# The end of a convolution in a two-layer backbone: its transforms, its adaLN units and its waits put in another order by hand

## The chip, the cores and the metric

The kernel runs on one core of one Trainium2 chip. The metric is device microseconds of one execution; a time shown is the median of the runs that it stands for. A core has a matrix engine (TensorE, PE in the profile, with its weight loads listed as PEld), a vector engine (VectorE, DVE), a scalar engine (ScalarE, ACT), a general engine (GpSimd, POOL) and an engine that here only issues loads (SyncE, SP). Each engine works through its own list of instructions in order. Matrix results land in PSUM, of which this kernel uses eight banks; everything else is in the on-chip memory SBUF, and weights come from device memory by DMA.

## The reference

The reference takes 256 latent tokens and 256 context tokens of width 1024 through two layers. Both layers have the form

```
sh1, sc1, g1, sh2, sc2, g2 = split(silu(c) @ ada_w[i] + ada_b[i], 6)      # adaLN
u = h * (1 + sc1) + sh1
h = LN(ALPHA * h + g1 * mixer(u))
h = LN(ALPHA * h + g2 * (relu(mod(h, sh2, sc2) @ w1) ** 2 @ w2))
```

for the latent stream with c and for the context stream with a learned vector. The mixer of layer 1 is a bidirectional mLSTM. The mixer of layer 0, where the change is, is a Conformer convolution:

```
a = u @ w_pw1 + b_pw1                     # 1024 -> 2048
a = a[:, :1024] * sigmoid(a[:, 1024:])
a = dwconv(a, w_dw)                       # 31 taps along the tokens; the latents in rows of 64
a = silu(LN(a + b_dw))
y = a @ w_pw2 + b_pw2
```

All inputs and outputs are float32.

## The kernel before

The 512 tokens are the columns of most tiles: context first, latents behind. A float32 product is made of three matmuls of shortened operands: each weight tile is split into a high part (a cast on ScalarE, L153) and a low part (a subtraction on VectorE, L154), and `mm3` (L175 to L180) multiplies high by high, high by low and low by high.

A planner lays out the program. It goes through the instructions in the order in which the code states them, which is their priority, gives each to its engine when its own model of the times says that its inputs are there, and adds the waits. So an engine's list can differ from the order of the code. Two means steer it: `tc.issue_after(x)` puts what is stated inside the block behind instruction x on x's engine, and `tc.high_priority(-100)` makes a block less urgent. Tiles of a kind (a tag) share a fixed number of buffers; a tile waits until one is free. PSUM has three banks "mm", two "ln", one "fl" and two "cv". Weights arrive in `raw` (three buffers of 1 MB, L149).

The convolution runs as follows.

- **Start.** The first adaLN quantities and four of pw1's sixteen output blocks are made together, feature block by feature block (`start0` to `start2`). Loads and small results use `F`, five buffers of 128x512.
- **Tables.** A block of low priority builds sine tables (L650 to L690) on VectorE, loads the row `bdw` (L705), and defines `taps`, which loads the 31 taps of one half of the channels into an F buffer (L710) and makes their spectra Hc and Hs with two matmuls of 31 rows (L713).
- **pw1.** `gemm_steps` (L218) makes the other twelve blocks, m = 0 to 11, two to a 1 MB load. After block m it calls `pw1_next(m)`. An even m gives a gate (a sigmoid on ScalarE, L761). An odd m gives a value, which VectorE multiplies by the gate (L765); PE transposes the result (L768) and ScalarE copies it into A (L769). Eight of these blocks, counting the first four, make 1024 channels; channels 0 to 511 are complete after m = 3, the others after m = 11.
- **Spectral filter.** `spectral(h, tt)` takes half h of the channels and one of four tiles tt of 128 tokens: two forward transforms (L788 for the context tiles 0 and 1, L794 for the latent tiles 2 and 3, where each is a 64-row matmul and the two can share the array), four products with Hc and Hs on VectorE (L805, L806), and an inverse transform of four matmuls in two pairs of 64 columns (L826), then the bias on VectorE (L833) and token statistics (L834). In the profile a float32 matmul is two records, so a whole inverse transform is x8.
- **Token norm.** `token_norm(pair)` turns the statistics of two tiles into a scale and a shift with a chain of small operations on VectorE (L839 to L847), and ScalarE applies them to the four half tiles (L851).
- **silu.** `silu(s)` transposes the two tiles of a stream back (L903), applies the activation (L905) and splits the result; pw2 consumes it. The context stream comes first.
- **adaLN units.** The remaining adaLN columns of layer 0 come in units of 512 columns, 2 MB each, as 8 products of 32 columns of the array (`ada_mm`, L334; 16 records), each on one of four column groups that run side by side. `Ada` collects units in the bank "fl": `ada_g1` units 4 and 5, `ada_s2` units 6 to 9, with a copy to SBUF behind the last (L374) and a fold into place (`end`, L342, L379). Before the change unit 4 and 5 come at m = 3 and 5, units 6, 7 and 8 at m = 7, 9 and 11 and unit 9 behind pw1; the first half of unit 8 lies in four small tiles loaded early (L883).

Behind pw1, before the change, `pw1_epi` states the second half's tiles 0 and 1 and the norm of that pair, then come unit 9, the context's silu, tiles 2 and 3 with a part of the products held back behind the norm, and the norm of the second pair.

## Time and profile before

| what | value |
|---|---|
| median of 3 runs | 1713.19 us |
| lowest and highest of them | 1710.81 and 1713.68 us |
| profiled execution | 1711.69 us |
| its span in the profile | 1709.9 us |
| mean granted clock of PE | 0.996 |
| PE busy | 1680.3 us, 98% of the span |
| VectorE busy | 1032.3 us, 60% |
| ScalarE busy | 746.2 us, 44% |
| instructions | 22801 |

The profile is one execution. The span goes from its first to its last instruction; the time of the execution is a little longer. Matmuls are pipelined and their ends are modelled, so two of them may overlap in the list, and a busy PE is not PE at its peak. The chain of work that ended last is followed back from the last instruction, at each step to what released it or to the instruction ahead of it on its engine; in order of time each row gives the start, the length, the engine with the tile and line, and how many instructions were merged. In a timeline, brackets give the engine's idle time before the row and who ended it. The waits list who waited for whom: total, times, longest. SPq rows are DMA issues. In the rows of busy time by stretches, the clock is the share of full speed that was granted to PE. Line numbers are those of the kernel before.

### The profile page before, as it was taken

What the parts mean: (1) busy time and instruction counts of PE and PEld (TensorE: products, weight loads), DVE (VectorE), ACT (ScalarE), POOL (GpSimd) and SP (SyncE); (2) the same over time, 40 slices, a digit from 0 to 9 for tenths busy, and PEclk for the clock granted to TensorE, in tenths of its full rate; (3) what the DMA queues carried; (4) which work ended last, traced back from release to release, by engine and by line L of the source; (5) the groups of instructions that cost most, each with busy time, mean ns of one, the idle gap of its engine ahead of it and who ended that gap; (6) DMA issues with size and microseconds to landing.
All of it is one profiled execution on the core that took longest, in us unless ns stands there. A gap on an engine that the chain in (4) does not pass through costs nothing.

```text
span 1709.9 us, 22801 instructions
## 1 busy us (share of the span) xinstructions
PE 1680.3 (98%) x8886; PEld 1365.5 (80%) x8886; DVE 1032.3 (60%) x1840; ACT 746.2 (44%) x1198; POOL 44.3 (3%) x92
## 2 busy tenths in 40 slices
PE   7999999999999999999999999999999999999997
PEld 5655798887888998876688899888877878878886
DVE  5554785666645675762144554464387776776677
ACT  3312664232324366652232542442467564545453
POOL 0000000000000000000000000000011120000001
PEclk9999999999999999999999999999999999999999
DMA  8436224443423155568675753355454556766552
GB/s 346 169 123 225 77 75 172 147 143 123 148 105 124 50 163 189 182 220 278 231 227 173 248 190 123 130 203 179 138 207 154 197 194 208 257 222 225 193 181 91
DMA packets 70396, 300.53 MB, mean 176 GB/s; under 512 B 7123, under 2 KB 21971, under 8 KB 39825
## 3 DMA queue, kind: packets, MB, share of 16 engines
q1 hardware_dynamic: 52624, 284.39, 47.4%
q10 hardware_dynamic: 17664, 14.69, 2.6%
q8 instruction: 70, 1.15, 0.3%
q14 instruction: 38, 0.30, 0.0%
HBM read 283.32 MB, written 15.73 MB: 175 GB/s over the span
## 4 chain that ended last, share of the span: by engine, by line
PE 92%; DVE 4%; ACT 1%; issue 1%; DMA 1%; POOL 0%; SPq 0%; DVEq 0%; ACTq 0%; POOLq 0%
PE mm L176 17%; PE mm L179 17%; PE mm L180 17%; PE mm L189 7%; PE mm L190 3%; PE mm L205 3%; PE mm L206 3%; PE mm L207 3%; PE cv L207 2%; PE cv L205 2%; PE cv L206 2%; PE fl L334 2%; DVE wl L154 1%; PE cv L826 1%; PE fl L739 1%
## 5 line engine op out<-in xcount | busy, mean ns | idle before, releaser
L154 DVE TENSOR_TENSOR wl<-raw,wh 128x1024 fp32r<-128x1024 f32 x346 | 424.5, 1233 | 273.9 <-ACT wh L153 271.3
L153 ACT CAST wh<-raw 128x1024 fp32r<-128x1024 f32 x346 | 360.3, 1050 | 492.3 <-PE mm L179 256.8
L179 PE MATMUL mm<-u,wh 128*128 128x512 f32 (+1 forms) x824 | 297.1, 361 | 0.0
L176 PE MATMUL mm<-u,wh 128*128 128x512 f32 (+1 forms) x696 | 248.6, 358 | 0.8 <-ACT wh L153 0.5
L180 PE MATMUL mm<-u,wl 128*128 128x512 f32 (+1 forms) x696 | 246.9, 355 | 0.0
L179 PEld LDWEIGHTS mm<-u,wh 128*128 128x128 f32 x824 | 156.0, 189 | 22.9 <-issue 1.3
L176 PEld LDWEIGHTS mm<-u,wh 128*128 128x128 f32 x696 | 131.6, 190 | 30.1 <-issue 5.7
L180 PEld LDWEIGHTS mm<-u,wl 128*128 128x128 f32 x696 | 131.8, 189 | 19.3 <-issue 1.3
L176 PE MATMUL mm<-xm,wh 128*128 128x512 f32 x256 | 102.2, 399 | 0.0
L205 PE MATMUL mm<-wh,xl 128*128 128x512 f32 x256 | 101.4, 397 | 0.5 <-ACT wh L153 0.5
L206 PE MATMUL mm<-wh,xl 128*128 128x512 f32 x256 | 100.9, 394 | 0.0
L180 PE MATMUL mm<-xm,wl 128*128 128x512 f32 x256 | 99.9, 390 | 0.0
L207 PE MATMUL mm<-wl,xl 128*128 128x512 f32 x256 | 99.6, 392 | 0.0
L176 PE MATMUL mm<-hid,wh 128*128 128x512 f32 (+1 forms) x256 | 93.1, 364 | 0.0
L179 PE MATMUL mm<-hid,wh 128*128 128x512 f32 (+1 forms) x256 | 92.8, 363 | 0.0
L180 PE MATMUL mm<-hid,wl 128*128 128x512 f32 (+1 forms) x256 | 92.7, 362 | 0.0
L189 PE MATMUL mm<-x,wh 128*128 128x512 f32 x232 | 81.0, 398 | 0.8 <-DVE x L1649 0.8
L410 DVE SCALAR_TENSOR_TENSOR S<-ar,cs,S 128x512 f32<-128x512 f32 x56 | 40.8, 749 | 64.7 <-DMA ar<-ada_w 64.6
L179 PE MATMUL mm<-qq,wh 128*128 128x272 f32 x256 | 73.9, 289 | 0.0
L176 PE MATMUL mm<-qq,wh 128*128 128x272 f32 x256 | 73.5, 288 | 0.0
L180 PE MATMUL mm<-qq,wl 128*128 128x272 f32 x256 | 73.5, 288 | 0.0
L189 PE MATMUL mm<-u,wh 128*128 128x512 f32 x192 | 68.6, 399 | 0.0
(506 smaller groups left out, 3270.1 us busy)
## 6 DMA issues: line engine op xcount, KB each, us to landing
raw<-w SPq DMA_DIRECT2D x64, 1024.0 KB, 4.8
raw<-wo SPq DMA_DIRECT2D x32, 1024.0 KB, 4.9
raw<-ada_w SPq DMA_DIRECT2D x27, 1024.0 KB, 5.0
ar<-ada_w SPq DMA_DIRECT2D x80, 256.0 KB, 3.8
raw<-wv SPq DMA_DIRECT2D x16, 1024.0 KB, 7.3
raw<-wqT SPq DMA_DIRECT2D x16, 1024.0 KB, 5.2
raw<-wq SPq DMA_DIRECT2D x16, 1024.0 KB, 5.1
raw<-wk SPq DMA_DIRECT2D x16, 1024.0 KB, 4.9
```

The source lines that it names most:

```text
L153: c = nc.scalar.copy(hi, src)
L154: nc.vector.tensor_tensor(lo, src, hi.bitcast(F32), op=ALU.subtract)
L176: a = nc.tensor.matmul(ps, wh, xh, start=start, stop=False)
L179: nc.tensor.matmul(ps, wh, xl, start=False, stop=False)
L180: nc.tensor.matmul(ps, wl, xh, start=False, stop=stop)
L189: todo = [lambda s_, e_: nc.tensor.matmul(ps, wh, r[0], start=s_, stop=e_), lambda s_, e_: nc.tensor.matmul(ps[:, :n], wl, r[0][:, :n], st ...
L190: lambda s_, e_: nc.tensor.matmul(ps[:, :n], wl, r[0][:, :n], start=s_, stop=e_)]
L205: nc.tensor.matmul(ps, xh, wh, start=start, stop=False)
L206: nc.tensor.matmul(ps, xl, wh, start=False, stop=False)
L207: nc.tensor.matmul(ps, xh, wl, start=False, stop=stop)
L334: a = nc.tensor.matmul(ps[32 * j:32 * j + 32], cs[:, kt, 14 - 2 * v:46 - 2 * v], blocks[kt], start=first and kt < 4, stop=last and kt >= 4 ...
L410: nc.vector.scalar_tensor_tensor(a, w, c, a, op0=ALU.mult, op1=ALU.add)
```

## The change

It leaves the arithmetic as it is, but for the engine that does two steps, and orders the work around the end of the convolution.

- The two tap loads move out of `taps` into the low-priority block of tables.
- `spectral` is taken apart into `fwd`, `products` (one half tile's two products a call) and `back`. For the first half of the channels they are called in the old order.
- For the second half the order is written out behind pw1: the first half of unit 9 behind the last transposes, the forward transforms of tiles 0 and 1, the inverse of 0 behind them, the forward of 2, the inverse of 1, the norm of the pair, the second half of unit 9. Within the silu of the context follow the second products of tile 2 behind the norm, its inverse and the forward of 3 behind the fourth transpose, and the inverse of 3 behind the sixth.
- Unit 4 is done in two halves around the transposes of m = 3; units 5, 6 and 7 come at m = 4, 6 and 8, each behind the last matmul of that block.
- The copy of `ada_s2` goes from VectorE to ScalarE. The token norm is applied to the pair's second tile by VectorE, to the first by ScalarE.

```diff
+    wds = [F()[:NTAP, :] for _ in range(2)]
+    for h_ in range(2):
+        nc.sync.dma_start(wds[h_], wdw_d[0:NTAP, h_ * 512:(h_ + 1) * 512])
     def taps(h_):
-        wd = F()[:NTAP, :]
-        nc.sync.dma_start(wd, wdw_d[0:NTAP, h_ * 512:(h_ + 1) * 512])
+        wd = wds[h_]
...
+                if self is ada_s2:
+                    nc.scalar.copy(self.sb, self.ps)
+                else:
+                    nc.vector.tensor_copy(self.sb, self.ps)
...
         if f == 3:
+            with tc.issue_after(mark["tr"]):
+                ada_g1.mm(first, range(4, 8))
             for tt in range(4):
-                spectral(0, tt)
-        if f == 7:
-            for tt in range(2):
-                spectral(1, tt)
-            token_norm(0)
+                fwd(0, tt, [psum() for _ in range(2)])
+                products(0, tt)
+                products(0, tt)
+                back(0, tt, psum("cv"))
...
-            for i in range(2):
-                y = Y[2 * pair + i][h]
-                nc.scalar.activation(y, y, AF.Identity, scale=mv[:, i, 2:3], bias=mv[:, i, 3:4])
+            y, z = [Y[2 * pair + i][h] for i in range(2)]
+            nc.scalar.activation(y, y, AF.Identity, scale=mv[:, 0, 2:3], bias=mv[:, 0, 3:4])
+            mark["norm", h] = nc.vector.tensor_scalar(z, z, mv[:, 1, 2:3], mv[:, 1, 3:4], op0=ALU.mult, op1=ALU.add).ins
...
     def pw1_next(m, ps):
+        if m == 3:
+            first.extend(ada_load(0, 4))
+            ada_g1.mm(first, range(4))
...
-        if m in Z.fd[:2]:
-            ada_g1.mm(ada_load(0, 4 + ada_g1.n))
-        if m == Z.fd[2]:
+        if m in (4, 6, 8):
+            unit = ada_g1 if m == 4 else ada_s2
+            blocks = ada_load(0, unit.u0 + unit.n)
+            with tc.issue_after(lastmm[0]):
+                unit.mm(blocks)
+        if m == 5:
             ada_g1.end()
-        if m in (7, 9):
-            ada_s2.mm()
-        if m == 9:
+        if m == 8:
...
     last = ada_load(0, 6 + ada_s2.n)
-    with tc.issue_after(mark["fwd", 1, 0]):
-        ada_s2.mm(last)
+    with tc.issue_after(mark["tr"]):
+        ada_s2.mm(last, range(4))
+    for tt in range(2):
+        fwd(1, tt, [psum() for _ in range(2)])
+    cv = [psum("cv") for _ in range(2)]
+    products(1, 0)
+    products(1, 0)
+    with tc.issue_after(mark["fwd", 1]):
+        back(1, 0, cv[0])
+    products(1, 1)
+    products(1, 1)
+    xb = [psum() for _ in range(2)]
+    fwd(1, 2, xb)
+    with tc.issue_after(mark["fwd", 2]):
+        back(1, 1, cv[1])
+    products(1, 2)
+    token_norm(0)
+    with tc.issue_after(mark["fwd", 2]):
+        ada_s2.mm(last, range(4, 8))
...
-    lead2 = [psum() for _ in range(2)]
-    banks = [psum(), psum("cv"), psum("cv")]
-    for tt in (2, 3):
-        spectral(1, tt, banks)
+    lead2 = [psum(), psum("cv")]
+    ob = psum("cv")
+    with tc.issue_after(mark["norm", 0]):
+        products(1, 2)
+    with tc.issue_after(mark["turn", 3]):
+        back(1, 2, ob)
+        fwd(1, 3, xb)
+    products(1, 3)
+    products(1, 3)
+    with tc.issue_after(mark["turn", 5]):
+        back(1, 3, ob)
     token_norm(1)
     ada_s2.end()
```

`mark["tr"]` is the last transpose of a value block, `mark["turn", f]` the last transpose of feature block f in the silu, `mark["fwd", tt]` the last forward matmul of a tile, and `lastmm[0]` the matmul that `mm3` stated last.

More of the change, by code (lines that the diff above doesn't have):

```diff
@@ L32 @@
 class Z:
-    fd = [3, 5, 6]
     wq0 = 2
@@ L179, in mm3 @@
         nc.tensor.matmul(ps, wh, xl, start=False, stop=False)
-        nc.tensor.matmul(ps, wl, xh, start=False, stop=stop)
+        lastmm[0] = nc.tensor.matmul(ps, wl, xh, start=False, stop=stop).ins
+    lastmm = [None]
     def mm_any(ps, wh, wl, r, start, stop):
@@ L329, in hybrid_kernel, with ada_mm @@
     ada = [con.tile([P, 48, 2], F32, name=f"ada{l}") for l in range(2)]
-    def ada_mm(ps, blocks, v=0, first=True, last=True):
-        for kt in range(DT):
+    def ada_mm(ps, blocks, v=0, first=True, last=True, kts=range(DT)):
+        for kt in kts:
             j = kt % 4
@@ L364, in __init__, with mm @@
             self.l, self.u0, self.nu, self.n = l, u0, nu, 0
-        def mm(self, blocks=None):
+        def mm(self, blocks=None, kts=range(DT)):
             n = self.n
-            if n == 0:
+            if n == 0 and 0 in kts:
                 self.ps = psum("fl")
-            ada_mm(self.ps, blocks or ada_load(self.l, self.u0 + n), n, n == 0, n == self.nu - 1)
+            ada_mm(self.ps, blocks or ada_load(self.l, self.u0 + n), n, n == 0, n == self.nu - 1, kts)
+            if DT - 1 not in kts:
+                return
             self.n += 1
@@ L373, in mm @@
                 self.sb = tmp("F")
-                nc.vector.tensor_copy(self.sb, self.ps)
+                if self is ada_s2:
+                    nc.scalar.copy(self.sb, self.ps)
+                else:
+                    nc.vector.tensor_copy(self.sb, self.ps)
         def end(self):
@@ L767, in pw1_epi, with fwd @@
         for b in range(4):
-            nc.tensor.transpose(tr[:, b * P:(b + 1) * P], a[:, b * P:(b + 1) * P], ident)
+            mark["tr"] = nc.tensor.transpose(tr[:, b * P:(b + 1) * P], a[:, b * P:(b + 1) * P], ident).ins
         nc.scalar.copy(A[:, :, f * P:(f + 1) * P], tr.rearrange("p (b c) -> p b c", b=4))
         if f == 3:
+            with tc.issue_after(mark["tr"]):
+                ada_g1.mm(first, range(4, 8))
             for tt in range(4):
-                spectral(0, tt)
-        if f == 7:
-            for tt in range(2):
-                spectral(1, tt)
-            token_norm(0)
-    def spectral(h, tt, banks=None):
+                fwd(0, tt, [psum() for _ in range(2)])
+                products(0, tt)
+                products(0, tt)
+                back(0, tt, psum("cv"))
+    ps_ = {}
+    def fwd(h, tt, xfs):
         sl = slice(h * 512, (h + 1) * 512)
-        ps_ = []
-        xfs = banks[:2] if banks else [psum() for _ in range(2)]
-        prod = F if h == 0 or tt % 2 else lambda: tmp("E")
+        ps_[tt] = [], list(xfs[::-1])
         for b in (1, 0):
@@ L787, in spectral, with half_ @@
                 for i, (fm, t) in enumerate(w_):
-                    mark["fwd", h, tt] = nc.tensor.matmul(xfs[b], fm, A[0:fm.shape[0], t, sl], start=i == 0,
-                                                          stop=i == len(w_) - 1).ins
+                    a = nc.tensor.matmul(xfs[b], fm, A[0:fm.shape[0], t, sl], start=i == 0, stop=i == len(w_) - 1)
             else:
-                def fwd():
+                def half_():
                     r = slice(64 * b, 64 * b + 64)
@@ L796, in spectral, with products, back @@
                 if b:
-                    lead = fwd()
+                    a = lead = half_()
                 else:
                     with tc.issue_after(lead.ins):
-                        fwd()
-        def products():
-            for i, xf in enumerate(xfs[::-1]):
-                p1, p2 = prod(), prod()
-                nc.vector.tensor_tensor(p1, xf, Hc[:, sl], op=ALU.mult)
-                nc.vector.tensor_tensor(p2, xf, Hs[:, sl], op=ALU.mult)
-                ps_.insert(0, (p1, p2))
-                if i == 0:
-                    yield
-        todo = products()
-        if tt < 3 or not banks:
-            next(todo)
-        if banks:
-            with tc.issue_after(mark["norm"]):
-                for _ in todo:
-                    pass
-        else:
-            next(todo, None)
-        o = banks[2] if banks else psum("cv")
+                        a = half_()
+        mark["fwd", tt] = a.ins
+    def products(h, tt):
+        sl = slice(h * 512, (h + 1) * 512)
+        done, todo = ps_[tt]
+        xf = todo.pop(0)
+        p1, p2 = [F() if h == 0 or tt % 2 else tmp("E") for _ in range(2)]
+        nc.vector.tensor_tensor(p1, xf, Hc[:, sl], op=ALU.mult)
+        mark["pr", tt] = nc.vector.tensor_tensor(p2, xf, Hs[:, sl], op=ALU.mult).ins
+        done.insert(0, (p1, p2))
+    def back(h, tt, o):
+        sl = slice(h * 512, (h + 1) * 512)
         for i, g_ in enumerate((G1, G2)):
@@ L825, in inv @@
                 def inv():
-                    return nc.tensor.matmul(o[r:r + 64, :], g_[:, r:r + 64], ps_[b][i], start=i == 0, stop=i == 1,
+                    return nc.tensor.matmul(o[r:r + 64, :], g_[:, r:r + 64], ps_[tt][0][b][i], start=i == 0, stop=i == 1,
                                             tile_position=(0, r))
@@ L846, in token_norm @@
             nc.vector.scalar_tensor_tensor(r, q, -1.5, r, op0=ALU.add, op1=ALU.mult)
-        mark["norm"] = nc.vector.scalar_tensor_tensor(q, m_, -1.0, r, op0=ALU.mult, op1=ALU.mult).ins
+        nc.vector.scalar_tensor_tensor(q, m_, -1.0, r, op0=ALU.mult, op1=ALU.mult)
         for h in range(2):
-            for i in range(2):
-                y = Y[2 * pair + i][h]
-                nc.scalar.activation(y, y, AF.Identity, scale=mv[:, i, 2:3], bias=mv[:, i, 3:4])
+            y, z = [Y[2 * pair + i][h] for i in range(2)]
+            nc.scalar.activation(y, y, AF.Identity, scale=mv[:, 0, 2:3], bias=mv[:, 0, 3:4])
+            mark["norm", h] = nc.vector.tensor_scalar(z, z, mv[:, 1, 2:3], mv[:, 1, 3:4], op0=ALU.mult, op1=ALU.add).ins
     pre2 = {}
@@ L885, in pw1_next @@
             pw2_raw.extend(raw_load(pw2[g, 0]) for g in range(2))
-    half = []
+    first, half = [], []
     warm = con.tile([P, 1], F32, name="warm")
@@ L902, in silu @@
             for i in range(2):
-                nc.tensor.transpose(xn[:, i * P:(i + 1) * P], Y[2 * s + i][f // 4][:, f % 4 * P:f % 4 * P + P], ident)
+                mark["turn", f] = nc.tensor.transpose(xn[:, i * P:(i + 1) * P],
+                                                      Y[2 * s + i][f // 4][:, f % 4 * P:f % 4 * P + P], ident).ins
             y = tmp("S")[:, LO]
```

## The prediction, made before the changed kernel was seen

> **What bounds the kernel now.** I read the page first, then the chain of work that ended last from 59 to 200 us, then TensorE's waits, then busy time and granted clock by stretches, and last the timelines of VectorE, ScalarE and the DMA queue there. The page:

> ```profile
> span 1709.9 us, 22801 instructions
> ...
> PE 92%; DVE 4%; ACT 1%; issue 1%; DMA 1%; POOL 0%; SPq 0%; DVEq 0%; ACTq 0%; POOLq 0%
> ```

> TensorE (PE) is 92% of the chain, so time is won where PE runs the same work in fewer slots, at a higher clock, or without a wait. The change touches the convolution, about 50 to 200 us. Its last part in the chain (start, length, both us):

> ```profile
> 153.69 1.85 PE fl L334 x16
> 155.54 0.60 PE ln L768 x4
> 156.17 0.59 ACT A L769
> 156.81 4.56 PE mm L788 x10
> 161.37 1.87 PE cv L826 x8
> 163.24 1.06 PE mm L788 x2
> ...
> 169.04 0.69 DVE F L374
> 169.73 0.60 DVE bst L834
> 170.33 0.59 DVE E L805
> ...
> 174.56 1.22 PE cv L826 x2
> 175.77 1.05 PE ln L903 x4
> 176.82 2.85 PE cv L826 x6
> 179.66 1.05 PE mm L794 x2
> ```

> L788 and L794 are the forward transforms, L826 the inverse ones, L334 the adaLN products, L768 and L903 transposes. The reader is to see that from 169 to 174.5 us the chain leaves PE for VectorE (DVE): the token norm of the first pair of tiles must end before the silu's transposes (L903) can begin. And an inverse transform takes 1.87 us as eight matmuls together, but 1.22 + 2.85 when it is split at 174.56.

> ```profile
> 59.30:62.71 3.41, 3.03 (x9) 1.00 0.49 176
> 62.71:66.12 3.41, 3.41 (x12) 0.50 0.04 16
> ...
> 171.94:175.35 3.41, 1.63 (x4) 1.00 0.37 154
> 175.35:178.76 3.41, 3.41 (x10) 0.50 0.00 0
> ```

> (Columns: the stretch, its length, PE's busy time, granted clock, share and rate of the DMA engines.) Twice in this region PE runs 3.41 us at clock 0.50, each time behind a stretch with little on the array: 59.30 to 62.71 holds a wait and four matmuls of 31 rows, 171.94 to 175.35 is half idle. A full stretch at half clock costs 3.41/2 = 1.7 us.

> **The change, part by part.** *adaLN units.* A unit is 8 products on four column groups, 16 matmul records. Its rows:

> ```profile
> 65.63 0.74 PE ln L768 x4
> ...
> 78.31 1.00 PE fl L334 x8
> ...
> 79.95 0.98 PE fl L334 x2
> ...
> 95.46 0.99 PE fl L334 x6
> ...
> 111.58 0.99 PE fl L334 x8
> ...
> 124.64 1.83 PE fl L334 x10
> 126.47 0.59 PE ln L768 x4
> 127.06 0.99 PE fl L334 x6
> ...
> 139.17 1.83 PE fl L334 x10
> ```

> Whole, a unit takes 1.85 (row at 153.69). Split 10 and 6, where a transpose cuts a group of four, it takes 1.83 + 0.99 = 2.82: 0.97 lost. Split 8 and 8 it loses nothing to speak of (0.99 each). Units 6 and 7 (124.64, and 139.17, cut alike) move behind an even block m, where no transpose follows, and are tied to the block's last matmul: 2 x 0.97. Unit 4 (78.31: 1.00 + 0.98 + 0.99 = 2.97) becomes two halves of 0.99: 0.99. Unit 5 was 8 and 8 already: nothing. Together 2.9. Against it, the transposes of the odd blocks now fall into the matmul stream; one that does so today took 0.74, 0.15 more than 0.59 (first row, partly at half clock; I count 0.07 each, bounds 0 and 0.15). **Term 1: -2.7** (-2.9 to -2.4). The ScalarE copy that these units covered at block 7 stays covered by the second half of unit 4. The loads keep their order in SP's queue; a unit used one block sooner frees its buffers sooner, so the loads behind it come no later.

> *Tap loads.* Two loads move ahead, into the table block.

> ```profile
> PE ln L713 <- DMA F<-wdw_d: 0.4, 1, 0.4
> ```

> The wait of 0.4 goes; next late is the sine table on DVE, which ends just before it. With the wait gone the stretch at 59.30 holds more matmuls of full rows, and the half clock behind it may go too: 0 to 1.7. I take half, as the stretch is near the limit. **Term 2: -1.2** (-0.4 to -2.1).

> [...]

> *The end.* Before, the first L903 was at 175.77. In the new order, from 155.54: transposes 0.60; half unit 0.99, which covers the copy of A (0.59) that PE idled for; all twelve forward records of tiles 0 and 1, 4.56 + 1.06; inverse 0, 1.87; forward 2 as a pair, 1.06; inverse 1, 1.87. That is 167.55. The DVE products that these wait for (0.6 each, four a tile) end some 0.5 to 1.5 us ahead of each inverse. The second half unit fills 0.99 behind it. Unit 9's copy goes to an idle ScalarE, so L374 (0.69) leaves DVE's path, and the second products of tile 2 are held behind the norm instead of standing ahead of it (L805 at 170.33). The norm:

> ```profile
> 169.65 0.68 DVE L834 BATCH_NORM_STATS2 bst<-u 128x6 f32<-128x512 f32 x1
> ...
> 171.51 0.16 DVE L841 TENSOR_SCALAR mv<-mv 128x2 f32<-128x2 f32 x1
> ...
> 173.94 2.93 ACT L851 ACTIVATE u<-u,mv 128x512 f32<-128x512 f32 x4 [17.18 <-DVE mv L847]
> ```

> From 167.55: 0.2 to DVE, bias add 0.69, statistics 0.68, aggregate 0.2, then L841 to L847 as before, 173.90 (where ScalarE's idle time ends) - 171.51 = 2.4: 171.7, 2.2 sooner. Then before, two of four ScalarE passes (2.93/4 = 0.73 each) and 0.37 more led to the transposes; now DVE does one of the two beside ScalarE (unseen at this shape; the DVE pass over 512 columns in L834 takes 0.68, so it hides): 0.04 + 0.73 + 0.37 = 1.14, instead of 1.87. First L903 at 172.85: 2.9 sooner. Behind it inverse 2 is whole, 1.87 instead of 2.85: 1.0 more. Forward 3 runs as a pair in the time that its second half took alone (1.05). Matmuls of pw2 and transposes are the same. So 3.9 at full clock.

> What the new order gives up: from 168.5 to 172.85 PE has only the fold of eight small matmuls (about 0.8, as at 118.25 below); it idles some 3.5 us, where before the longest pause was the 1.8 (3.41 - 1.63) in the stretch at 171.94.

> ```profile
> 118.25 0.79 PE fl L342 x8
> ```

> A stretch like that is emptier than the one at 171.94, so at least one stretch at half clock follows; before's own is within the 2.85. Added to the ledger above: 1.7 if it lies on inverses, none if it falls on waiting, 3.4 if two follow. I take one: **Term 3: -2.2** (-3.9 to -0.5).

> The wait that the hand order adds: inverse 3 and inverse 2 stand in PE's in-order queue, with pw2's matmuls behind them, and wait for DVE products that queue among the silu's splits; if the planned place is early, PE stands still up to four products, 4 x 0.6 = 2.4. Nothing in before's chain shows such a wait at inverse 3 (no row between 179.66 and pw2 is a wait), so I take 0, bound 2.4.

> *Sum:* -2.7 - 1.2 - 2.2 = -6.1. The profiled execution took 1711.69 us (span 1709.9 and 1.8 around it), 1.5 below the median of the runs shown, 1713.19. So 1705.6 on its scale, **1707.1** on the median's.

> **The rivals.** What a measurement of this kernel can tell is about 0.2%, 3.4 us: faster means below 1709.8.

> *1, the gap eats the end.* Two stretches at half clock (term 3 at -0.5), term 2 at its 0.4, and PE standing 1 to 2.4 us before inverse 2 or 3: -2.7 - 0.4 - 0.5 + 1.7 = -1.9, 1711.3. For it: PE idles longer than before, and behind the gap come transposes, then matmuls of 64 columns. Against: at 175.35 a stretch with the same mix was followed by full clock.

> [...]

> *2, it doesn't do what it says.* The tie to a block's last matmul is a lower bound in time only; if the planner still cuts units 4, 6 and 7, term 1 is gone: -3.4, 1709.8.

> *3, half unit 9 stands in front.* It now comes before the forward transforms, with all of PE's work behind it.

> ```profile
> 147.13 8.81 SPq L149 DMA_DIRECT2D raw<-ada_w  x2
> ...
> DMA to landing us min/median/max: 4.7/4.9/6.8
> ```

> Its load goes out at 147.13 and lands near 152.0, 4 us ahead of need. If the planner gave it the other half's place (issue ends at 155.94, lands 160.5) PE would wait 4.4 and lose a stretch, 1.7: 0.0 in all, 1713.2.

> *4, slower: the tap loads block SP's queue.* They draw on the five F buffers, which the start phase and the sine tables use as well.

> ```profile
> 35.03 4.62 SPq L149 DMA_DIRECT2D raw<-pw  x2
> 39.69 0.86 SPq L705 DMA_DIRECT2D bdw<-wdw_d  x1
> ...
> 53.10 3.03 SPq L710 DMA_DIRECT2D F<-wdw_d  x2
> ```

> Both taps were issued by 56.13. If a tap load stands ahead of 35.03 and waits for a buffer until then, pw1's first weights land at 61 (4.9 behind) and are split by 63.3 (2.27):

> ```profile
> 45.93 2.27 DVE wl L154 x2
> ```

> Before they were split by 48.20, so PE loses about 15 us: -6.1 + 15 = +9, 1722. It decides at 35.03: behind 39.69 it costs nothing, as what is loaded there (unit 4, used at 78.31) has over 15 us to spare. Against it: the load traced just before the taps (bdw) went out at 39.69.

> **How the numbers follow.** Forecast 0.60; rival 1 0.20; rival 2 0.06; rival 3 0.06; rival 4 0.08. Faster: 0.60 and half of rival 2, 0.63. Slower: rival 4, and 0.03 from rivals 1 and 3 with worse prices, 0.11. Same: the rest, 0.26. The low end is all terms at their best, -2.9 - 2.1 - 3.9 = -8.9, 1704.3, less 1.0 for the scatter of the three runs (1710.81 to 1713.68): 1703.3. The high end takes in rivals 1 to 3: 1713.5. Outside remain rival 4 and little else.

> **What would show it.** Right: units 4 to 9 as x16 or x8 and x8; no clock of 0.50 near 62 us; the first L903 6 to 7 us sooner than 175.77 in its execution (2.9, and terms 1 and 2); L826 as x8 everywhere at the end. Wrong: L334 still x10 and x6; PE waiting for the DVE products in front of L826 while pw2's matmuls stand ready; two stretches of 0.50 behind the norm; a wait of PE for raw<-ada_w at the first half of unit 9; raw<-pw issued later than 40 us.

## The result and the profile after

| | median | lowest to highest, runs |
|---|---|---|
| before | 1711.61 us | 1710.02 to 1714.14, 22 |
| after | 1709.54 us | 1706.64 to 1713.15, 22 |
| ratio | 0.9984 | 95% interval 0.9978 to 0.9991 |

The change is worth 2.07 us, 0.16%: real by its interval, and less than the 0.2% that the prediction held a measurement of this kernel able to tell. The forecast was 6.1 us less than before; rival 1 had said 1.9 less.

The page of the profile after. This execution took 1707.85 us, 3.84 less than the profiled one of before:

```profile
span 1706.0 us, 22804 instructions
...
PE 91%; DVE 5%; ACT 2%; issue 1%; DMA 1%; POOL 0%; SPq 0%; DVEq 0%; ACTq 0%; POOLq 0%
```

The chain is still PE's, a per cent less of it than before. Its rows over the end of the convolution (start, length, engine, tile, line, merged instructions; L335 are adaLN units, L797 and L802 forward and L827 inverse transforms, L925 the silu's transposes, L851 the norm's pass on ScalarE):

```profile
151.12 1.85 PE fl L335 x16
...
153.56 0.99 PE fl L335 x8
154.56 5.35 PE mm L797 x12
159.91 1.87 PE cv L827 x8
161.78 1.06 PE mm L802 x4
162.84 1.87 PE cv L827 x8
164.70 1.04 PE fl L335 x8
...
166.40 1.07 PE fl L343 x8
169.84 0.82 ACT u L851
170.71 0.70 PE ln L925 x2
...
174.94 2.31 PE cv L827 x6
177.25 0.59 PE ln L925 x4
177.84 1.00 PE cv L827 x2
178.84 1.11 PE mm L802 x4
179.95 0.67 DVE F L816
...
184.07 1.94 PE cv L827 x8
```

Up to the norm the order is the one written by hand: units whole (x16, or x8 and x8), forward 2 ahead of inverse 1, the norm ready at 169.8 where it was 173.9. Behind the transposes it isn't: inverse 2 is cut (x6, four transposes, x2), forward 3 comes only behind it, and the products of tile 3 and inverse 3 follow as a chain.

PE's waits from 38 to 200 us (who waits for whom: total, times, longest):

```profile
PE ln L925 <- ACT u L851: 3.2, 1, 3.2
PE ln L722 <- DMA F<-wdw_d: 0.7, 1, 0.7
PE fl L343 <- ACT F L378: 0.7, 1, 0.7
PE cv L827 <- DVE F L816: 0.6, 2, 0.5
PE mm L802 <- DVE F L817: 0.5, 1, 0.5
```

The wait on the tap rows is not gone; it is 0.7 where it was 0.4. And PE's busy time by stretches, cut where the granted clock changes (us, busy time of PE, PEld, DVE, ACT and POOL with their instructions, the clock, DMA):

```profile
165.59:169.00 3.41, 1.17 (x12) 0.97 (x8) 2.39 (x17) 0.58 (x1) 0.00 (x0) 1.00 0.61 207
169.00:172.41 3.41, 1.48 (x6) 1.00 (x6) 2.87 (x9) 2.47 (x4) 0.00 (x0) 0.50 0.24 101
172.41:175.83 3.42, 3.42 (x14) 2.07 (x13) 1.19 (x3) 2.50 (x7) 0.00 (x0) 0.50 0.00 0
```

Two stretches at half clock follow the gap, not one.

The rest of this document reads every profile at four landmarks of PE's timeline: the first matmul of unit 4, the first of unit 8 (just ahead of the last transposes), the first silu transpose, and the first pw2 matmul of the fifth output block, behind which the order of the work is nearly the same in all kernels. "62" and "170" give how long PE ran at half clock near these places.

| kernel | unit 4 | unit 4 to 8 | 8 to transpose | transpose to block 5 | 8 to block 5 | 62 | 170 |
|---|---|---|---|---|---|---|---|
| before | 78.23 | 75.39 | 22.07 | 20.34 | 42.41 | 3.41 | 3.41 |
| after | 78.32 | 72.72 | 19.66 | 23.00 | 42.66 | 3.41 | 6.83 |
| e1_units | 78.31 | 72.76 | 22.78 | 19.65 | 42.43 | 3.41 | 3.41 |
| e2_end | 76.94 | 75.38 | 19.66 | 22.86 | 42.52 | 0 | 6.83 |
| e3_fill | 78.86 | 73.06 | 18.66 | 21.47 | 40.13 | 3.41 | 0 |
| e4_fold_late | 77.06 | 72.72 | 18.65 | 22.85 | 41.50 | 0 | 6.83 |
| e5_taps | 83.41 | 72.71 | 19.66 | 22.94 | 42.60 | 0 | 6.83 |
| e6_whole | 81.28 | 72.75 | 18.65 | 23.20 | 41.85 | 6.83 | 6.83 |
| e7_gap | 77.32 | 72.74 | 20.60 | 22.19 | 42.79 | 0 | 6.83 |
| e8_all | 83.36 | 72.74 | 20.59 | 20.88 | 41.47 | 0 | 3.41 |
| e9_taps_mid | 75.85 | 72.71 | 19.67 | 23.59 | 43.26 | 0 | 6.83 |
| e10_gap_late | 80.30 | 72.73 | 18.66 | 22.35 | 41.01 | 6.83 | 6.83 |
| e11_all | 77.13 | 72.73 | 18.65 | 21.43 | 40.08 | 0 | 3.41 |
| e12_taps_alone | 77.22 | 75.41 | 22.28 | 20.14 | 42.42 | 0 | 3.41 |

So in the two first profiles the units gave 2.67, the taps nothing (0.09 lost), and the end, from unit 8 to block 5, lost 0.25: the first transpose 2.41 sooner, and 2.66 more behind it. Block 5 came 2.33 sooner. Another 1.24 comes between 224 and 290 us: a later adaLN unit, which the diff does not touch, is cut in two before and stands whole after (the chain before, then after):

```profile
236.99 0.98 PE fl L334 x2
269.11 1.85 PE fl L334 x14
```

```profile
265.54 1.85 PE fl L335 x16
```

The planner does this as a consequence of the change outside the units. In the profiles of e1_units and e12_taps_alone, which keep the old end, this unit is cut in the same way; in the other ten experiments it is whole, also in e2_end, which has all of the change but the units.

### The profile page after: what moved, and what is told of

It is laid out like the page before. It is cut to its first block, busy times and chain, and to the rows that moved or that the text cites. A ratio compares the mean times of both kernels' runs of the same rounds, so it can differ in the third digit from the quotient of the medians.

```text
span 1706.0 us, 22804 instructions
## 1 busy us (share of the span) xinstructions
PE 1675.0 (98%) x8886; PEld 1365.7 (80%) x8886; DVE 1035.2 (61%) x1843; ACT 744.6 (44%) x1195; POOL 44.3 (3%) x92
## 4 chain that ended last, share of the span: by engine, by line
PE 91%; DVE 5%; ACT 2%; issue 1%; DMA 1%; POOL 0%; SPq 0%; DVEq 0%; ACTq 0%; POOLq 0%
PE mm L175 17%; PE mm L178 17%; PE mm L179 17%; PE mm L190 7%; PE mm L191 3%; PE mm L208 3%; PE mm L206 3%; PE mm L207 3%; PE cv L208 2%; PE cv L207 2%; PE cv L206 2%; PE fl L335 1%; DVE wl L153 1%; PE fl L748 1%; PE ln L175 1%
## 5 line engine op out<-in xcount | busy, mean ns | idle before, releaser
L178 PE MATMUL mm<-u,wh 128*128 128x512 f32 (+1 forms) x808 | 293.1, 363 | 0.0
L175 PE MATMUL mm<-u,wh 128*128 128x512 f32 (+1 forms) x680 | 245.5, 361 | 0.7 <-ACT wh L152 0.5
L179 PE MATMUL mm<-u,wl 128*128 128x512 f32 (+1 forms) x680 | 242.4, 357 | 0.0
L178 PEld LDWEIGHTS mm<-u,wh 128*128 128x128 f32 x808 | 153.2, 190 | 23.4 <-issue 1.5
L175 PEld LDWEIGHTS mm<-u,wh 128*128 128x128 f32 x680 | 129.3, 190 | 29.2 <-issue 8.2
```

Of the source, the lines that this page charges most:

```text
L175: a = nc.tensor.matmul(ps, wh, xh, start=start, stop=False)
L178: nc.tensor.matmul(ps, wh, xl, start=False, stop=False)
L179: lastmm[0] = nc.tensor.matmul(ps, wl, xh, start=False, stop=stop).ins
```

## The experiments

Two theories for the end. **A**: the emptier gap in front of the transposes costs half clock, and this alone ate the gain. **B**: what stands behind the transposes, cut and chained, ate it whatever the clock. Each kernel was compared with the kernel before on the same chip.

**One part alone, on the kernel before and on the changed one.** e1_units: units 4 to 7 moved and unit 4 halved as in the change, with their loads, nothing else.

```diff
+        if m in (4, 6, 8):
+            unit = ada_g1 if m == 4 else ada_s2
+            blocks = ada_load(0, unit.u0 + unit.n)
+            with tc.issue_after(lastmm[0]):
+                unit.mm(blocks)
```

> Kernel before with the adaLN units 4 to 7 moved and whole, nothing else of the change. Both theories: units 5, 6, 7 as x16 and unit 4 as x8 and x8 in the profile, so -2.7 us against before (the changed kernel's trace has -2.65 by the first matmul of unit 8). Theory A (the end's gain is eaten by half clock behind a longer idle stretch of PE) and theory B (it is eaten by waits and cut pairs in PE's list behind the transposes) both say that the end is worth about nothing, so this kernel should time within 1 us of the changed one; if the end by itself still gives the 2.2 us that was forecast, this one is 2 us slower than the changed one.

1711.51 us, ratio 1.0004 (0.9995 to 1.0013). The trace has what was expected of it: 2.63 less from unit 4 to unit 8, and PE 2.54 ahead of before until 1140 us. Then 0.4 is lost, and 1.4 more from 1261 us on, where there is a stretch at half clock that before does not have:

```profile
1257.55:1260.96 3.41, 2.76 (x12) 1.34 (x11) 3.00 (x6) 3.35 (x5) 0.00 (x0) 1.00 0.11 23
1260.96:1264.37 3.41, 3.41 (x9) 2.63 (x9) 1.43 (x4) 3.38 (x7) 0.73 (x1) 0.50 1.00 299
```

PE ends 0.68 ahead. A gain can be real where it is made and be gone at the end of the program; the ratio's interval allows 0.9 us of gain at most. And the median is 2.0 above the changed kernel's, which is what was expected if the end by itself still gave its 2.2 us, and not by theory A or B.

e2_end: the changed kernel with the units put back to m = 3, 5, 7 and 9 (unit 8 at 11).

```diff
-        if m in (4, 6, 8):
+        if m in (3, 5):
+            ada_g1.mm(ada_load(0, 4 + ada_g1.n))
...
+        if m in (7, 9):
+            ada_s2.mm()
```

> The changed kernel with units 4 to 8 back at the blocks m = 3, 5, 7, 9 and 11, untied and not halved: the end's new order alone, with the tap loads. Forecast as it stood: -2.2 (-3.9 to -0.5) against before. Theory A: 0, plus or minus 1; the first transpose of the silu stands about 2.4 us sooner than before, and it is followed by two stretches of clock 0.50 instead of one. Theory B: 0 as well, but whatever the clock does; the profile then has PE waits before the inverse transforms of 1 us or more.

1709.67 us, ratio 0.9989 (0.9981 to 0.9998). From unit 8 to block 5 it takes 42.52, before 42.41: the end by itself gives nothing there. It is 1.4 ahead of the changed kernel at unit 4, since in this execution no half clock follows the wait on the tap rows, which the two kernels load alike. Two stretches of half clock follow the gap, as theory A had it; the wait of 1 us or more before an inverse, theory B's sign, is not there (0.5). The median is 1.9 under before's, more than either expected. In this profile 1.3 us come from the half clock that is missing near 62 us, and 1.24 from the later unit.

So the medians divide the change otherwise than the landmarks do: nothing for the units alone, 1.9 for all but the units, 2.07 for both. The landmarks tell what happens in a place of one execution, and the sum of such places is not the median.

**The gap and the norm.** e4_fold_late: the changed kernel, with VectorE's addition of the adaLN fold (L385) ordered behind the norm's last pass.

```diff
-    ada_s2.end()
+    with tc.issue_after(norm0):
+        ada_s2.end()
```

The reason is VectorE's timeline in the changed kernel (start, length; in brackets its idle time and who ended it):

```profile
166.45 0.17 DVE L842 TENSOR_SCALAR mv<-mv 128x2 f32<-128x2 f32 x1
167.50 0.19 DVE L385 TENSOR_TENSOR ada<-fl,vecs 128x32 f32<-128x32 f32 x1 [0.88 <-PE fl L343]
167.61 0.16 DVE L843 TENSOR_SCALAR mv<-mv 128x2 int32<-128x2 int32 x1
```

L385 stands in the middle of the norm and waits for the fold on PE, which waits for the copy on ScalarE; L843 to L848, the rest of the norm, stand behind it.

> The changed kernel with the fold of units 6 to 9 taken into place (L385 and what follows from it on VectorE) held behind the norm of the first pair. In the changed kernel's list it stands second in the norm's chain and waits 0.9 us for PE's fold and ScalarE's copy. Both theories: the norm ends 0.7 to 0.9 sooner and so do the first transposes. Theory A: -0.4 to -0.8 against the changed kernel, half of what is won being spent at half clock. Theory B: -0.7 to -0.9.

1707.96 us, ratio 0.9976 (0.9966 to 0.9986). The first transpose is 1.01 sooner (18.65 against 19.66), and PE's wait for the norm falls by as much:

```profile
PE ln L926 <- ACT u L851: 2.2, 1, 2.2
```

Behind the transposes it takes 22.85 us, as before this edit (23.00), so the microsecond reaches block 5 (41.50 against 42.66). The median is 1.6 under the changed kernel's, but the intervals of the two ratios overlap.

e3_fill: the same, with 13 matmuls of 128x512 behind unit 9 whose result nobody reads.

```diff
+    idle = psum()
+    with tc.issue_after(mark["ada"]):
+        for _ in range(13):
+            nc.tensor.matmul(idle, kcol(pre2[0], 0)[0], u[7][0], start=True, stop=True)
```

> The last kernel (fold late) with 13 matmuls of 128x512 more behind unit 9, whose result nobody reads: about 2.9 us of work put into the stretch where PE idles. They add work and do nothing else. Theory A: the stretches of clock 0.50 behind 168 us go, or one of them, and the kernel is 1.5 to 2.5 us faster than the one without the extra matmuls. Theory B: the same time within 0.5, or slower where an extra matmul stands before the first transpose.

1709.37 us, ratio 0.9986 (0.9977 to 0.9995). Its stretches over the end:

```profile
165.69:169.10 3.41, 3.41 (x19) 2.16 (x12) 3.02 (x12) 0.59 (x1) 0.00 (x0) 1.00 0.39 111
169.10:172.52 3.42, 2.89 (x18) 2.05 (x17) 3.15 (x10) 2.68 (x5) 0.00 (x0) 1.00 0.47 196
```

Full clock throughout, and the time behind the transposes falls from 22.85 to 21.47. So in its place theory A is right for 1.4 us, a little less than the 1.5 to 2.5 that it expected. The median does not show it: it is 1.4 above e4's. The profiled execution had half clock at 62 us, where e4's had none, and lost 1.1 more between 800 and 1000 us; why the other runs are slower is not shown.

At full clock the end behind the transposes still takes 1.1 more than before's 20.34, though 3.1 us of that ran at half clock. PE's records between these two landmarks show what is more: 16 records of inverse transforms where before has 14, 4 of forward transforms where it has 2, and 1.0 us of idle time where it has none (0.7 in e4). In the kernel before, the missing records stand ahead of the first transpose. This is theory B's part.

**What stands behind the transposes.** e6_whole: e4 with the transposes of f = 4 to 7 ordered behind inverse 2's last matmul.

```diff
+                with tc.issue_after(mark["inv"] if f == 4 and s == 0 and i == 0 else mark["norm", 0]):
+                    mark["turn", f] = nc.tensor.transpose(...)
```

> The late fold (DVE's addition of adaLN behind the norm), and inverse 2's eight matmuls kept in one piece: the transposes of f = 4 to 7 are ordered behind its last matmul instead of between the sixth and the seventh. Theory A (only the half clock ate the end): the time from the first silu transpose to the first matmul on hid stays at the 22.85 us of the late fold alone; median 1708.0. Theory B (waits and cuts behind the transposes ate it): that time falls by the 0.9 us that the cut costs, to about 21.9; median 1707.0, ratio 0.9972. Rival C: the transposes that now stand behind feed ScalarE later and the gain is lost again: 22.5 to 23.5.

1707.57 us, ratio 0.9976 (0.9967 to 0.9985). Rival C: 23.20 us behind the transposes, nothing gained. The chain shows why:

```profile
176.78 2.75 PE cv L827 x8
...
182.81 1.07 PE cv L827 x2
183.89 0.37 PE ln L927 x2
184.26 1.86 PE cv L827 x6
```

Inverse 2 is whole, and the transposes held back by it now cut inverse 3. A whole inverse 2 is not a gain that can be added to a sum.

e7_gap: e4 with tile 3's forward transform in PE's gap behind unit 9, with banks of its own.

```diff
+    xc = [psum("cv"), psum()]
+    with tc.issue_after(mark["ada"]):
+        fwd(1, 3, xc)
...
-    lead2 = [psum(), psum("cv")]
+    lead2 = [xb[1], xb[0]]
-        fwd(1, 3, xb)
```

> The late fold, and tile 3's forward transform moved from behind inverse 2 into PE's gap behind the whole-width unit 9's last half, with banks of its own (one cv, one mm; the first pw2 products then take the two banks of tile 2's forward). Theory A (half clock only): two more matmuls in the gap do not keep the clock; first silu transpose to first hid matmul 22.85 less the 1.1 us that the two matmuls took there at half clock, 21.8; median 1707. Theory B (chain of waits: forward 3, products 3, inverse 3 follow one another behind the transposes): the products of tile 3 start sooner as well, PE's wait before inverse 3 (0.5) goes, 21.2 to 21.5; median 1706.3, ratio 0.9968. Rival C: the fifth group's bank comes free later: no gain, 1708.

1708.10 us, ratio 0.9978 (0.9969 to 0.9987). Behind the transposes 22.19, 0.66 less; but the first transpose came 1.95 later than in e4, which no theory had said. The chain:

```profile
165.67 0.17 DVE mv L845
165.84 0.66 DVE F L818
...
166.57 0.60 DVE F L819
...
167.90 0.60 DVE F L819
```

With its inputs ready early, the planner puts tile 3's four products (L818, L819; 165.84 to 168.50) between the norm's small instructions. It is the mistake of L385 again, ahead of which VectorE idled for 0.88 us with the rest of the norm behind it: VectorE takes these rows in the list's order, and here 2.66 us of products stand in front of the rest of the norm. The 1.1 us that theory A counts for forward 3 at half clock were at full clock: in e4 it starts at 176.41 and takes 1.11, and half clock ends near 173.2.

e10_gap_late: e7 with these products ordered behind the norm.

```diff
+    with tc.issue_after(norm0):
+        products(1, 3)
+        products(1, 3)
```

> The late fold and forward 3 in the gap, with tile 3's four products ordered behind the first norm, so that they cannot stand among the norm's small instructions on VectorE. If those products were what ate forward 3's gain: the time from unit 8 to the first silu transpose falls from 20.60 back to 18.65 us, and from the transpose to the first hid matmul it stays at 22.2 or falls to 21.2; the sum is 40.0 to 40.9 (41.50 with the late fold alone, 42.66 in the changed kernel); median 1706.9, ratio 0.9973. Rival: the products, now behind the norm, come late for inverse 3 and the sum stays at 41.5: median 1708.0.

1707.54 us, ratio 0.9975 (0.9964 to 0.9985). The first transpose is back at 18.66 and behind it are 22.35: 41.01 from unit 8 to block 5, half a microsecond under e4's in this place, at the same 6.83 us of half clock. The sum is just above the 40.0 to 40.9 expected; the median is 0.4 under e4's, which these runs cannot tell from none.

**The tap rows.** SP's issues in the changed kernel (start, length):

```profile
34.75 4.61 SPq L148 DMA_DIRECT2D raw<-pw  x2
42.09 6.19 SPq L148 DMA_DIRECT2D raw<-ada_w  x2
48.33 0.43 SPq L711 DMA_DIRECT2D bdw<-wdw_d  x1
52.40 0.33 SPq L148 DMA_DIRECT2D raw<-pw  x1
52.83 3.03 SPq L716 DMA_DIRECT2D F<-wdw_d  x2
```

They go out at 52.83; before it was 53.10. Their line moved inside a block of low priority, so the raw loads, stated later, still go first and hold SP while they wait for buffers; the first tap load follows the raw load at 52.40 directly. The second then waits 2.7 us more for a buffer of `F`. e5_taps: the changed kernel with the two rows in a tile of their own, loaded at the program's start.

```diff
+    wdt = padp.tile([P, D], F32, name="wdt")
+    nc.sync.dma_start(wdt[:NTAP, :], wdw_d[0:NTAP, :])
```

> The changed kernel, with one part of it really done: the two tap rows get a tile of their own and are loaded at the program's start, ahead of the weight loads of the start loop, instead of into two F tiles behind the raw loads. Theory (step T2 was costed rightly but the load did not move): PE's wait of 0.7 us on the tap rows goes, nothing takes its place, and the first unit behind it starts 0.7 us or more sooner by the trace than in the changed kernel (78.32 us); median 0.5 to 1.5 us under the changed kernel's 1709.54, so about 1708.5 and a ratio of 0.998. Rival: the load at the start goes ahead of the first weights and costs what it saves: the same start of the unit, ratio 0.9985 to 0.999. The clock of 0.50 near 63 us stays or goes by where the throttle's grid falls in this execution, by either theory.

1713.51 us, ratio 1.0013 (1.0004 to 1.0022): slower. PE's first wait from 0 to 80 us, of this kernel and then of the changed one:

```profile
PE fl L335 <- DMA raw<-ada_w: 13.5, 1, 13.5
```

```profile
PE fl L335 <- DMA raw<-ada_w: 6.4, 1, 6.4
```

124 KB ahead of everything made the first weights 7.1 us late, far more than the rival had allowed. But of 7.47 us at 58.6 us only 5.09 are left at unit 4: wait and half clock near 62 us are gone, 2.4 us, the most that step T2 could bring.

e9_taps_mid: the same tile, loaded behind the start loop and ahead of the block of low priority.

```diff
+    wdt = padp.tile([P, D], F32, name="wdt")
+    nc.sync.dma_start(wdt[:NTAP, :], wdw_d[0:NTAP, :])
     later = tc.high_priority(-100)
```

> The changed kernel with the tap rows loaded into a tile of their own right behind the start loop's loads, ahead of the raw loads that wait for their buffers, at SP's normal priority. If only the place of the load was wrong: the start stays (first unit behind the taps no longer 5.1 us late as with the load at the program's start), PE's wait of 0.7 us on the tap rows is gone, and the first unit starts at 77.6 us or, where the half clock near 63 us goes as well, at 75.9 (78.32 in the changed kernel); median 0.7 to 2.4 us under its 1709.54, so about 1708. Rival: the 4-KB rows hold up the loads behind them wherever they stand, and the first unit starts later than 78.3.

1707.66 us, ratio 0.9973 (0.9962 to 0.9985), 1.9 under the changed kernel by medians, though the intervals overlap. The load goes out at 29.27, the start is as it was, PE's waits have no row for the taps, and unit 4 starts at 75.85, 2.47 sooner. Of that 0.6 is lost again behind the silu's transposes (23.59 against 23.00).

e12_taps_alone: this edit alone on the kernel before.

> The kernel before with the tap rows alone moved: a tile of their own, loaded behind the start loop's loads at SP's normal priority. Step T2 by itself, as the prediction meant it (1.2 us, between 0.4 and 2.1): PE's wait on the tap rows (0.4) goes, the first unit behind them starts at 77.8 us or, where the half clock at 62 us goes too, at 76.1 (78.23 before), and everything behind keeps that difference to the end: median 1711.0 to 1709.5, ratio 0.9988 to 0.9995. Rival (the clock's grid alone makes the difference, the wait has nothing to do with it): a stretch of 0.50 stands near 62 us though PE no longer waits, and the first unit starts at 77.8.

1711.09 us, ratio 0.9999 (0.9990 to 1.0008). Unit 4 starts 1.01 sooner, although PE is 0.96 behind at 58 us; the step is worth 2.0 in its place, near its upper bound. (About half of the 0.96 is there at 20 us already: full clock was granted from 20.58 us on, and in before from 18.34.) PE stays 1.0 ahead until 960 us; then 0.7 goes, and 1.3 at 1263 us, with a stretch of half clock as in e1, and PE ends 1.0 behind. The step's size is right in the place where it acts, and nothing is left of it at the end of this execution.

**All together.** e8_all: e7, e6's order and e5's load at the start.

> All together: the late fold, inverse 2 in one piece, forward 3 in the gap, and the tap rows loaded at the start. If the parts add up: 0.9 and 1.4 us in the end and 0.7 at the taps under the late fold's 1707.96, so 1705.0, ratio 0.9962, first silu transpose to first hid matmul 20.5 us. If the half clock behind the gap rules (theory A), the end gives only forward 3's 1.1: 1706.2, ratio 0.9969. Rival: with inverse 2 whole and forward 3 gone from behind it, PE stands for tile 3's products before inverse 3 for 1 us more, and the whole is worth no more than forward 3 alone.

1713.59 us, ratio 1.0007 (0.9998 to 1.0016): the start cost of e5 and the late transpose of e7 are both in it, and none of the expectations had either. Behind the transposes it takes 20.88, with one stretch of half clock.

e11_all: e10 and e9's load.

> The late fold, forward 3 in the gap with late products, and the tap rows behind the start loop. If the parts add: 1.6 us at the taps (between 0.7 and 2.4), and 40.0 to 40.9 us from unit 8 to the first hid matmul: 2.5 us under the late fold alone, about 1705.5, ratio 0.9964. Rival: the half clock falls elsewhere in its place and the sum of the parts is not seen: 1707 to 1708.

1705.35 us, ratio 0.9956 (0.9943 to 0.9970), the fastest kernel of the study: 7.0 us under before's median in the same runs, 1712.32. From unit 8 to block 5 it takes 40.08, and PE's longest wait from 38 to 200 us is

```profile
PE ln L930 <- ACT u L852: 2.0, 1, 2.0
```

Its interval lies below the changed kernel's (0.9978 to 0.9991). This is the gain that was forecast for the change and a little more, after three further edits: the tap rows ahead of the raw loads, the fold and tile 3's products behind the norm, forward 3 in the gap. It is not made of the forecast's terms alone, as the later unit's 1.24 is in it. The profiled execution is 7.3 ahead of before's until 1500 us and then loses 1.3 with a stretch of half clock at 1511.5, so single executions do not tell it from e4 (1705.35 and 1705.41).

## Where the prediction was right and where it was wrong

The time, 1709.54, lies inside the stated range, but the gain is a third of the forecast: 2.07 for 6.1. The forecast of 1707.1 is only 2.4 off because it started from three runs of before with a median of 1713.19, and 22 runs have 1711.61; those 1.6 us are luck.

**Term 1, units whole, was right in its place**: 2.67 in the changed profile, 2.63 in e1, for 2.7. In the medians it isn't seen: e1 has the time of before.

**Term 2, the tap loads, failed at its first step.** The prediction took the loads to go out ahead, in the block of tables; they went out 0.3 sooner than before. It looked for the danger that they stand ahead of the raw loads (rival 4) and not for the chance that they stay behind them. The price was right in its bounds, and higher than the 1.2 that was taken: wait and half clock are worth 2.0 us on the kernel before (e12) and 2.4 on the changed one (e5, e9), whose wait is 0.7 and not 0.4; the bound was 2.1. That the stretch at 59.30 is "near the limit", for which half of the 1.7 was taken, was the author's estimate: no run shows a limit. In the five profiles without the wait (e5, e8, e9, e11 and e12) no half clock came near 62 us.

**Term 3, the end, failed in three of its steps.** The forecast was 2.2, from 3.9 at full clock and 1.7 for one stretch of half clock; from unit 8 to block 5 the change lost 0.25. At full clock, and with L385 out of the way, it gains 2.28 there (e3, 40.13 against 42.41), not 3.9.

- "First L903 at 172.85: 2.9 sooner": 2.41. The prediction followed the norm's chain but not what else stands in VectorE's list among it; L385 costs 1.0 there (e4). Without it the step would have given 3.4.
- "Behind it inverse 2 is whole ... 1.0 more": it is cut as before, and keeping it whole gains nothing, as the transposes then cut inverse 3 (e6). At full clock the time behind the transposes is 1.1 longer, not 1.0 shorter (e3). Two records of an inverse and two of a forward transform that stood ahead of the transposes now stand behind them, and forward 3, its products and inverse 3 come one after another there. The wait that the prediction named as the risk of the hand order was short (0.6 in two, for a bound of 2.4); the cost was work left for after the norm while PE stood idle ahead of it. e10 took back 0.5.
- "I take one" stretch of half clock: there were two, as rival 1 had it. Full clock instead of two is worth 1.4 (e3), less than the 1.7 that the prediction counts for a single one. With one instead of two, e11 is 0.9 faster than e10 over the same stretch of work (40.08 and 41.01).

**Rival 1 is what happened**: two stretches, and the tap wait's half clock still there. That its sum, 1.9 less than before, is close to the measured 2.07 is luck in part: PE did not stand 1 to 2.4 us before the inverses, and the 1.24 us of the later unit were in no sum.

The chance of 0.20 for rival 1 was too low for what was on the table: the prediction itself had found that PE would idle longer than before any half clock that the trace showed.

What stays open: why the units alone and the taps alone, 2.5 and 1.0 us ahead in the middle of their profiles, end with no gain in the medians, while the change without the units (e2) has nearly the median of the whole change. In the profiles of e1 and e12 a stretch of half clock near 1261 us takes 1.3 to 1.4 of the lead; whether it comes as often in the other runs of these kernels isn't shown, and the 0.4 and 0.7 us lost ahead of it have not been traced to a row. So the steps above are shown for places of single executions, and the share of each in the median is not.

## What to carry to other kernels

A hand order for one engine is only as good as the lists of the others: follow VectorE's list through a chain of short dependent instructions, and hold back by an explicit tie everything that could be ready there (L385 cost 1.0 us, tile 3's products 1.95). A load that moves in the code has moved only when its row in SP's issues has; in a block of low priority it still stands behind what is stated later (52.83 us here, where it was 53.10). And where the matrix engine waits for a chain, move real work into the wait rather than behind it, since the gap is paid for a second time in half clock (1.4 us here, by e3).

## What the runs showed of the hardware

**A cell need not be idle.** In e1 PE was busy for 2.76 of 3.41 us and lost the clock; in the changed kernel at 62 us, 2.74:

```profile
59.76:63.17 3.41, 2.74 (x8) 1.39 (x9) 0.87 (x1) 1.44 (x3) 0.00 (x0) 1.00 0.32 117
63.17:66.58 3.41, 3.41 (x12) 2.73 (x11) 1.98 (x2) 1.26 (x2) 0.00 (x0) 0.50 0.18 32
```

What these two have in common is a pause and matmuls on few rows:

```profile
60.43 1.95 PE L722 MATMUL ln<-F,tab 31*128 31x512 f32 x4 [0.75 <-DMA F<-wdw_d]
```

```profile
1258.87 0.68 PE L1389 MATMUL ln<-negm,ident 36*128 36x256 f32 x2
```

Without the wait, in e9, the cell with the four matmuls of 31 rows (58.46 to 61.88) was busy for 3.39 us and full clock stayed.

**Busy time alone doesn't part the cells.** In before PE was busy for 3.03 us in the cell at 59.30, and half clock followed; in the cell at 1516.83 it was busy for 2.05, and full clock stayed. The second one, by stretches and by groups of PE's lines in the first of them (busy time, mean ns; idle time ahead):

```profile
1516.83:1520.24 3.41, 2.05 (x13) 1.71 (x14) 3.17 (x11) 2.33 (x8) 0.00 (x0) 1.00 0.68 234
1520.24:1523.66 3.42, 3.42 (x22) 2.95 (x21) 3.29 (x12) 3.42 (x12) 0.00 (x0) 1.00 0.99 395
```

```profile
L1634 PE MATMUL ln<-ident,res 128*128 128x128 f32 x8 | 1.1, 279 | 1.3 <-DVE res L1602 1.3
```

Of its 2.05 us 1.08 are transposes of 128 rows. In the changed kernel the cells ahead of the two stretches near 170 us were busy for 1.17 us (165.59, without a transpose) and 1.48 (169.00, with transposes), and half clock followed both. What matmuls on few rows, transposes and idle time each do to the granted clock is not shown: no run takes them apart.
